# Two loads of the first expert layer: from SyncE's queue to GpSimd's

## The chip, the cores and the metric

The kernel runs on one core of one Trainium2 chip. The metric is the device time of one execution in microseconds. Before the change it is 3697.25 us, the median of three runs (3697.02 to 3698.64).

## What is computed

The reference runs two blocks of two layers each over 256 tokens of 1024 values. The part that matters here is the expert stage (`peer_ffn`) of the first block. Each token picks, for each of 8 heads, 16 of 16384 experts; expert e has a row `u[e]` and a row `v[e]`, and the stage adds `sum over the picked e of gate(t, e) * gelu(x(t) . u[e]) * v[e]`. In the first layer it runs for 512 tokens (256 of the sequence, 256 of the context), in the second for 256.

```
q = (xc @ w_q).reshape(PEER_CHUNK, PEER_HEADS, 2, PEER_HALF)
...
top_s, pos = lax.top_k(cand, PEER_TOPK)
eidx = jnp.take_along_axis(cidx, pos, axis=-1)
gate = jax.nn.softmax(top_s, axis=-1)
u = u_emb[eidx]
hid = jax.nn.gelu(jnp.einsum('td,thkd->thk', xc, u))
wgt = (gate * hid.astype(jnp.float32)).astype(xc.dtype)
return jnp.einsum('thk,thkd->td', wgt, v_emb[eidx])
```

## The kernel before, in words

**Dense and gathered tokens.** In the first layer 384 of the 512 tokens take the dense way: the hidden values of all 16384 experts are computed and multiplied with a matrix of gates that is zero where an expert wasn't picked. The other 128 tokens (NROW) take the gathered way, class `Rows`: their 16 x 8 picked rows of u, and later of v, are fetched one vector of 128 rows at a time by an indirect DMA on GpSimd's (POOL's) queue (`fetch`, line 258, 512 KB each). There are 128 fetches of u-rows, each followed by a dot product on DVE (L274), and then 128 fetches of v-rows, each pair followed by eight small matmuls on TensorE into `ps_row` (L307). There are five row buffers (ROWBUFS). Each fetch is made to wait for the matmul that was issued last at its place in the program (`pace_by`, `beat`), so that it goes out with TensorE's progress. In the second layer there are no gathered tokens, and `self.rows` is None there.

**Jobs.** The dense way goes through 64 jobs of 256 experts. A job needs the hidden values `hs` (128 x 768 for 384 tokens), the gates G for the same experts, and 1 MB of v weights. For 42 jobs (NLEAD) hs is computed early, while the picks are made, and stored to DRAM (`lead`, `hd`). The gates are built as one-hot products and stored to DRAM in blocks of 32 tokens (`gd`). The values loop then runs over the jobs: `prep` loads hs (L1209) or computes it from 1 MB of u weights (`hidden`, 22 jobs), multiplies it with G and splits the product into Wh and Wl on ScalarE and DVE; `values` multiplies these with the v weights (L1269). Jobs come in pairs, in turn a computed and a loaded one until the computed ones are used up, then loaded ones alone. One load of G (`gates`, L1556) serves a pair of jobs. In the first layer it moves 768 KB in runs of 512 bytes; there are 32 such loads, the first of which (704 KB, before `self.gcur` is set) is issued on POOL's queue in both layers and the rest on SP's.

**Buffers.** hs, G, Wh and Wl have two buffers each. Weights go through raw buffers (`wload`, L351): two, and in this loop a third. A raw buffer is free again when ScalarE has made the high part and DVE the low part of both its halves (L361, L362). The weights of the next stage's modulation pass through the same buffers (L624).

**What sets the order.** The program is written as one sequence; a planner at build time puts each engine's instructions in an order by its own estimate of when their operands are ready, and adds waits on semaphores. Each engine, and each queue of DMA issues, then works in that order. SP issues nothing but DMAs, and before the change its queue holds the u, v and modulation weights and the loads of hs and G. All SP transfers are in DMA queue q1 of the trace, POOL's in q0, and ScalarE's in q10.

Of the kernel before, what the change touches and what calls it, by code (L numbers as in the profile page):

```python
# [329 lines left out]
class Prog:  # L330
# [869 lines left out]
    def prep(self, l, b, xh, xl, T, gd, hd):  # L1200

        nc = self.nc
        G = self.gates(l, b, gd, T // GSTAGE, T)
        hs = self.hsp.tile([P, 2, T], F32, tag="hs", name="hs_r", bufs=2)
        if b >= NLEAD[l]:
            for _ in self.hidden(l, b, xh, xl, T, hs):
                pass
        else:
            nc.sync.dma_start(hs, hd[b])  # L1209
        Wh = self.pp.tile([P, 2, T], F32R, tag="Wh", name="Wh", bufs=2)  # L1210
        Wl = self.pp.tile([P, 2, T], F32R, tag="Wl", name="Wl", bufs=2)
        w = hs.rearrange("p j (q t) -> p j q t", t=GSTAGE)
        nc.vector.tensor_tensor(w, w, G.rearrange("p q j t -> p j q t"), op=ALU.mult)  # L1213
        self.split(Wh, Wl, hs)
        return Wh, Wl
# [334 lines left out]
    def gates(self, l, b, gd, nq, T):  # L1550
        nc = self.nc
        key = (l, b // 2)
        if self.gcur is None or self.gcur[0] != key:
            G = self.pp.tile([P, nq, 4, GSTAGE], F32, tag="G", name="G", bufs=2)
            n = nq if self.gcur else nq - 1
            (nc.sync if self.gcur else nc.gpsimd).dma_start(G[:, :n].rearrange("p q j t -> p q (j t)"),  # L1556
                              gd[:n, :, (b // 2) * 4:(b // 2) * 4 + 4, :].rearrange("q p j t -> p q (j t)"))
            if n < nq:
                nc.gpsimd.tensor_copy(G[:, n], self.glast)
            self.gcur = (key, G)  # L1560
        return self.gcur[1][:, :, (b % 2) * 2:(b % 2) * 2 + 2, :]
# [367 lines left out]
```

## Time and profile before

| what | value |
|---|---|
| median of the runs | 3697.25 us |
| the profiled execution | 3701.45 us, of which the span of instructions is 3699.7 us |
| TensorE (PE) busy | 3574.0 us, 97% of the span, 21681 matmuls |
| DVE, ScalarE (ACT), POOL busy | 2461.5, 1634.3, 604.0 us |
| DMA | 777.60 MB, mean 210 GB/s |
| q1 (SP), q0 (POOL), q10 (ScalarE), share of 16 engines | 43.7%, 10.4%, 5.0% |
| chain that ended last | PE 41%, DVE 4%, DMA 2%, the rest below that |
| mean granted TensorE clock | 0.985 of full speed |

The values loop of the first layer lies between 1190 and 2100 us of the span. In a row of the timeline, the first number is the start in us and the second the duration, and the bracket is the idle time of the engine before it and what ended it. In a row of the table of groups, the numbers behind the bar are busy time in us, mean ns of one, and idle time before. A granted clock of 1.00 is 2.4 GHz.

### The profile page before, as it was taken

The numbers are of one execution on the slowest core, as the hardware profiler recorded it, in microseconds if no ns is written. First come the engines' busy times: TensorE is split into PE (matmuls) and PEld (weight loads), VectorE is DVE, ScalarE is ACT, GpSimd is POOL, SyncE is SP. The second block draws the span as 40 slices with busy tenths as digits, with TensorE's granted clock in tenths as the row PEclk, the third lists the DMA queues.
The fourth block names the chain that finished last, engine by engine and source line by source line (L and its number), as shares of the span: only waits on it lengthen the run. The fifth ranks groups of instructions, "written<-read, shape, count | busy, mean of one in ns | idle before, by whom it ended". The sixth has DMA issues, their size and how long they took to land.

```text
span 3699.7 us, 55016 instructions
## 1 busy us (share of the span) xinstructions
PE 3574.0 (97%) x21681; PEld 3097.0 (84%) x21681; DVE 2461.5 (67%) x4540; ACT 1634.3 (44%) x2608; POOL 604.0 (16%) x686
## 2 busy tenths in 40 slices
PE   7999999899999998999999999999999999999999
PEld 5988877789999877776766799999998888887787
DVE  5566556599697777744445677778876555557675
ACT  3334333336576322222222354555676444445454
POOL 0112222100011232322222121221000000002121
PEclk9999999999999999999999999999999999999999
DMA  5222145224689898888889533354578766766453
GB/s 212 75 86 80 69 154 216 75 83 170 228 323 336 315 332 306 325 295 309 298 321 325 188 115 120 120 175 160 200 269 292 244 236 237 242 231 212 145 174 111
DMA packets 227763, 777.60 MB, mean 210 GB/s; under 512 B 17296, under 2 KB 100752, under 8 KB 168496
## 3 DMA queue, kind: packets, MB, share of 16 engines
q1 hardware_dynamic: 165984, 567.29, 43.7%
q0 software_dynamic: 37184, 135.41, 10.4%
q10 hardware_dynamic: 24336, 71.38, 5.0%
q8 instruction: 170, 2.79, 0.3%
q14 instruction: 89, 0.73, 0.1%
HBM read 705.60 MB, written 68.42 MB: 209 GB/s over the span
## 4 chain that ended last, share of the span: by engine, by line
PE 41%; DVE 4%; DMA 2%; ACT 1%; issue 1%; POOL 1%; DVEq 0%; ACTq 0%; SPq 0%; POOLq 0%
PE keep L1269 12%; PE ps_mm L393 5%; PE ps_mm L395 5%; PE ps_mm L394 5%; PE ps_wide L395 2%; PE ps_wide L393 2%; PE ps_wide L394 2%; PE ps_v L1269 1%; DVE ulo L362 1%; PE ps_nar L393 1%; PE ps_nar L395 1%; PE ps_nar L394 1%; DMA wraw<-in_v 1%; PE ps_mm L414 1%; PE ps_row L307 1%
## 5 line engine op out<-in xcount | busy, mean ns | idle before, releaser
L361 ACT ACTIVATE uhi<-wraw 128x1024 fp32r<-128x1024 f32 x586 | 609.0, 1057 | 879.2 <-PE ps_mm L394 336.1
L393 PE MATMUL ps_mm<-xh,uhi 128*128 128x256 f32 (+2 forms) x2952 | 955.5, 324 | 9.2 <-ACT hs L1566 3.7
L395 PE MATMUL ps_mm<-xh,ulo 128*128 128x256 f32 (+2 forms) x2952 | 940.8, 319 | 7.1 <-DVE ulo L362 7.1
L362 DVE TENSOR_TENSOR ulo<-wraw,uhi 128x1024 fp32r<-128x1024 f32 x586 | 718.0, 1237 | 340.6 <-ACT uhi L361 317.6
L394 PE MATMUL ps_mm<-xl,uhi 128*128 128x256 f32 (+2 forms) x2952 | 939.9, 318 | 0.0
L393 PEld LDWEIGHTS ps_mm<-xh,uhi 128*128 128x128 f32 x2952 | 562.5, 191 | 54.0 <-issue 9.2
L395 PEld LDWEIGHTS ps_mm<-xh,ulo 128*128 128x128 f32 x2952 | 562.2, 191 | 29.4 <-DVE ulo L362 8.0
L394 PEld LDWEIGHTS ps_mm<-xl,uhi 128*128 128x128 f32 x2952 | 562.7, 191 | 20.8
L362 DVE TENSOR_TENSOR vlo<-wraw,vhi 128x1024 fp32r<-128x1024 f32 x184 | 224.0, 1222 | 187.7 <-ACT vhi L361 187.5
L361 ACT ACTIVATE vhi<-wraw 128x1024 fp32r<-128x1024 f32 x184 | 193.2, 1056 | 338.1 <-DMA wraw<-in_v 176.0
L1269 PE MATMUL keep<-vlo,Wh 128*128 128x512 f32 x656 | 256.7, 391 | 3.6 <-DVE vlo L362 3.6
L1269 PE MATMUL keep<-vhi,Wh 128*128 128x512 f32 x656 | 257.8, 393 | 0.5 <-ACT Wh L422 0.5
L1269 PE MATMUL keep<-vhi,Wl 128*128 128x512 f32 x656 | 256.2, 391 | 0.3 <-DVE Wl L423 0.3
L258 POOL DMA_INDIRECT row<-in_urow,eu x128 | 158.5, 1238 | 589.7 <-PE ps_mm L395 440.7
L1213 DVE TENSOR_TENSOR hs_r<-hs_r,G 128x768 f32<-128x768 f32 (+1 forms) x128 | 105.2, 823 | 170.7 <-DMA hs_r<-hd 106.9
L393 PE MATMUL ps_nar<-uhi,xh 128*128 128x256 f32 x704 | 201.3, 286 | 2.3 <-ACT cs L664 2.3
L394 PE MATMUL ps_nar<-ulo,xh 128*128 128x256 f32 x704 | 200.1, 284 | 0.0
L395 PE MATMUL ps_nar<-uhi,xl 128*128 128x256 f32 x704 | 199.9, 284 | 0.0
L258 POOL DMA_INDIRECT row<-in_vrow,ev x128 | 136.0, 1063 | 375.4 <-PE keep L1269 180.2
L1530 ACT ACTIVATE stage<-ps_g 128x512 f32<-128x512 f32 x160 | 165.1, 1160 | 1.7 <-DMA wraw<-in_u 0.8
L274 DVE CUSTOM_DVE_ANT_0 row<-row,xt 128x1024 f32<-128x1024 f32 x128 | 155.2, 1219 | 4.5 <-DMA row<-in_urow,eu 4.5
L1269 PEld LDWEIGHTS keep<-vhi,Wh 128*128 128x128 f32 x656 | 123.7, 189 | 36.8 <-issue 9.2
(428 smaller groups left out, 6965.2 us busy)
## 6 DMA issues: line engine op xcount, KB each, us to landing
wraw<-in_u SPq DMA_DIRECT2D x128, 1024.0 KB
wraw<-in_v SPq DMA_DIRECT2D x128, 1024.0 KB
wraw<-in_wa SPq DMA_DIRECT2D x104, 1024.0 KB
wraw<-in_wb SPq DMA_DIRECT2D x50, 1024.0 KB
gd<-stage ACTq DMA_DIRECT2D x80, 512.0 KB
wraw_m<-in_wmod SPq DMA_DIRECT2D x24, 1024.0 KB
G<-gd SPq DMA_DIRECT2D x31, 768.0 KB
mraw<-in_wmod SPq DMA_DIRECT2D x16, 1024.0 KB
```

The source lines that it names most:

```text
L258: ins = self.nc.gpsimd.indirect_dma_start(row, None, self.p.g[name], bass.IndirectOffsetOnAxis(ap=idx, axis=0))
L274: ins = nc.vector.tensor_tensor_reduce(out=row, in0=row, in1=self.xt, op0=ALU.mult, op1=ALU.add, scale=1.0, scalar=0.0, accum_out=self.hid ...
L307: nc.tensor.matmul(ps[c:c + 32, :], m[:, g, :], rows[n - 4 + g][:, h * 512:(h + 1) * 512], start=(i == 0), stop=(i == 31), tile_position=( ...
L361: nc.scalar.activation(hi, r, AF.Copy)
L362: nc.vector.tensor_tensor(lo, r, hi.bitcast(F32), op=ALU.subtract)
L393: nc.tensor.matmul(ps, lh, rh, start=(i == 0), stop=False)
L394: nc.tensor.matmul(ps, lh, rl, start=False, stop=False)
L395: self.beat = nc.tensor.matmul(ps, ll, rh, start=False, stop=(i == n - 1))
L414: self.nc.tensor.matmul(ps[:, t0:t1], a[:, s], b[:, k, t0:t1], start=(n == 0 and i == 0), stop=(n == KD - 1 and i == 2))
L1213: nc.vector.tensor_tensor(w, w, G.rearrange("p q j t -> p j q t"), op=ALU.mult)
L1269: self.beat = self.nc.tensor.matmul(ps, a[:, j, t], b[:, c], start=(start and j == 0 and i == 0), stop=(stop and j == 1 and i == 2), skip_ ...
L1530: nc.scalar.activation(st[:, :, tb:tb + 4].rearrange("p j t -> p t j"), pg, AF.Copy, scale=1.0 / GSCALE)
```

## The change

Two issues go from SP's queue to POOL's where there are gathered tokens, that is in the first layer alone: the load of the early hidden values hs (42 loads of 384 KB) and the load of the gates G (the 31 loads of 768 KB that were SP's). The weights stay on SP. The second layer is as before.

```
@@ prep
         else:
-            nc.sync.dma_start(hs, hd[b])
+            (nc.gpsimd if self.rows else nc.sync).dma_start(hs, hd[b])
@@ gates
-            (nc.sync if self.gcur else nc.gpsimd).dma_start(G[:, :n].rearrange("p q j t -> p q (j t)"),
+            (nc.sync if self.gcur and not self.rows else nc.gpsimd).dma_start(G[:, :n].rearrange("p q j t -> p q (j t)"),
                               gd[:n, :, (b // 2) * 4:(b // 2) * 4 + 4, :].rearrange("q p j t -> p q (j t)"))
```

## Rows read from the trace of the kernel before

**Rows 1.** Table of stretches: us, engines' busy us, clock, DMA share, GB/s
```profile
1190.00:1600.00 410.00, 380.35 (x1817) 322.60 (x1816) 290.33 (x393) 122.28 (x150) 127.09 (x104) 0.96 0.87 317
1600.00:2100.00 500.00, 490.81 (x2417) 343.14 (x2416) 239.12 (x328) 131.71 (x153) 131.77 (x126) 0.99 0.86 305
```

**Rows 2.** Timeline of PE, first and last stall of the first half
```profile
1273.98 0.69 PE L393 MATMUL ps_mm<-xh,vhi 128*128 128x384 f32 x1 [4.47 <-DVE racc L1236]
...
1578.67 0.42 PE L393 MATMUL ps_mm<-xh,vhi 128*128 128x384 f32 x1 [3.13 <-ACT uhi L361]
```

**Rows 3.** Timelines of DVE and ACT at the first stall, and a later load
```profile
1256.30 0.96 DVE L1213 TENSOR_TENSOR hs_r<-hs_r,G 128x768 f32<-128x768 f32 x1 [2.59 <-DMA hs_r<-hd]
...
1269.88 2.00 ACT L361 ACTIVATE uhi<-wraw 128x1024 fp32r<-128x1024 f32 x2 [9.23 <-DMA wraw<-in_v]
...
1585.82 1.06 ACT L361 ACTIVATE vhi<-wraw 128x1024 fp32r<-128x1024 f32 x1 [2.16 <-DMA wraw<-in_v]
```

**Rows 4.** Timeline of SP's issues before the first and the last stall
```profile
1248.46 0.33 SPq L1209 DMA_DIRECT2D hs_r<-hd  x1
...
1257.29 0.37 SPq L1556 DMA_DIRECT2D G<-gd  x1
1261.85 0.35 SPq L351 DMA_DIRECT2D wraw<-in_v  x1
...
1561.53 0.37 SPq L1556 DMA_DIRECT2D G<-gd  x1
1564.94 0.33 SPq L351 DMA_DIRECT2D wraw<-in_u  x1
...
1580.83 0.33 SPq L351 DMA_DIRECT2D wraw<-in_v  x1
```

**Rows 5.** Waits of SP's queue, 1190 to 2110: us in total, times, longest
```profile
SPq L1556 <- DVE hs_r L1213: 120.0, 20, 8.9
SPq L1209 <- DVE Wl L423: 112.7, 26, 10.1
```

**Rows 6.** DMA queues, 1257 to 1262 us: packets, MB, share of 16 engines
```profile
DMA packets 1831, 1.74 MB, mean 348 GB/s; under 512 B 47, under 2 KB 1602, under 8 KB 1830
...
q1 hardware_dynamic: 1570, 0.80, 58.1%
q0 software_dynamic: 260, 0.93, 48.6%
```

**Rows 7.** DMA queues, 1190 to 1200 us, with POOL's one G
```profile
DMA packets 1048, 3.98 MB, mean 398 GB/s; under 512 B 113, under 2 KB 113, under 8 KB 979
...
q0 software_dynamic: 480, 1.77, 47.5%
```

**Rows 8.** Timelines: two gathers on POOL, and who waited for them
```profile
1288.85 1.71 POOL L258 DMA_INDIRECT row<-in_urow,eu  x1 [0.30 <-issue]
...
1298.05 1.23 DVE L274 CUSTOM_DVE_ANT_0 row<-row,xt 128x1024 f32<-128x1024 f32 x1 [2.37 <-DMA row<-in_urow,eu]
...
1671.37 1.38 POOL L258 DMA_INDIRECT row<-in_vrow,ev  x1 [1.36 <-PE keep L1269]
...
1682.20 1.06 PE L307 MATMUL ps_row<-row,mask 128*32 128x512 f32 x6 [0.65 <-DMA row<-in_vrow,ev]
```

**Rows 9.** Groups by line, POOL
```profile
L258 POOL DMA_INDIRECT row<-in_vrow,ev x128 | 136.0, 1063 | 375.4 <-PE keep L1269 180.2 <-PE ps_v L1269 87.3 <-PE ps_mm L395 81.2
```

**Rows 10.** POOL's G of the second layer: its issue, and q0 from 2832.7 to 2838
```profile
2828.54 1.07 POOL L1556 DMA_DIRECT2D G<-gd  x1 [235.11 <-PE ps_g L1528]
...
q0 software_dynamic: 128, 0.46, 28.8%
```

**Rows 11.** Timelines of POOL and PE near the end of the loop
```profile
1999.73 1.40 POOL L258 DMA_INDIRECT row<-in_vrow,ev  x1 [2.94 <-PE keep L1269]
...
2008.85 1.06 PE L307 MATMUL ps_row<-row,mask 128*32 128x512 f32 x8
```

**Rows 12.** DMA issues from 1586 to 2110 us: count, KB each
```profile
G<-gd SPq DMA_DIRECT2D x18, 768.0 KB
```

## The prediction

> **What bounds the kernel now.** I read the table of stretches over the values loop of the first layer first, because the two edited lines act only there (1190 to 2100 us). The reader is to see two halves [rows 1]. From 1190 to 1600 us, where the rest of the hidden values is computed and the u-rows are fetched, TensorE is idle for 410 - 380.35 = 29.7 us, and its granted clock averages 0.96: part of the time it stands at 1.2 GHz instead of 2.4, which loses another 0.04 x 410 = 16.4 us. From 1600 to 2100 us it is idle for 9.2 us and the clock is 0.99. So what faster loads can give lies in the first half: 29.7 us, and at most 16.4 us of clock on top.
>
> Next, TensorE's timeline, for who ended the idle times. There are six stall places in the first half, one in every four jobs; the first lasts 4.47 us, the last ends with 3.13 us [rows 2]. Some name a DVE add on racc, some the split of a weight. DVE and ScalarE at the first place show that both are one thing: ScalarE waits 9.23 us for a v weight [rows 3], DVE, which works in order, waits for ScalarE, and so can't free the accumulator. SyncE's timeline shows the late weight [rows 4]: the v load was issued at 1261.85, 4.2 us after a load of G (1257.29 + 0.37), and was used at 1269.88, 8.0 us after its issue. A v load with no G just ahead took from 1580.83 to 1585.82, 5.0 us [rows 3, 4]. All six places have a G issued 1 to 5 us ahead of the late weights, as in the first (1257.29, 1261.85) and the last (1561.53, 1564.94) [rows 4].
>
> **What the change does, part by part.** Sums are made against the profiled execution, 3701.45 us, which lies 4.2 us over the median of 3697.25 us; the difference is taken off at the end.
>
> *Removed from SP:* 42 issues of hs and 31 of G. SP's wait for the buffer of G was 120.0 us in 20 cases and for that of hs 112.7 us in 26 cases [rows 5]. One would expect the weights behind them to gain that. They don't: after the wait for G that ended at 1257.29 the weight still waited until 1261.85 for its own raw buffer. I take 0 for the issue waits; the bounds are 0 and the 29.7 us of idle time, as more can't be given back.
>
> *Weights no longer behind G in the transfer queue (q1).* While G moves, q1 has 1570 packets in 5 us, nearly all of the 512-byte kind (under 2 KB less under 512 B is 1555), and they fill 58.1% of 16 engines: 0.581 x 5 us x 16 / 1570 = 30 ns each [rows 6]. A whole G is 768 KB, 1536 of them, 2.9 us of all engines, which it shares with the gathered rows in q0. A weight issued behind G waits for it. Without G it should take between 5.0 and 8.0 us; as the rows, and G itself in q0, still compete, I take 2.0 of the 3.0 us. Six places: -12 us (bounds 0 and -18). If the stalls get shorter, some stretches at 1.2 GHz go too: I take -3 us (bounds 0 and -16.4).
>
> *G in q0.* The one G of this layer that POOL issues already moves without any packet between 512 B and 2 KB: q0 has 480 packets in 10 us at 47.5%, 158 ns each, 3.7 KB on average [rows 7]. 768 KB in packets of 4096 B are 192, or 192 x 158 / 16 = 1.9 us. So G costs 1 us less of the DMA engines, 31 us over 910 us; I count it as part of the 2.0 us above. G's own landing has time: its buffer becomes free when the pair of jobs before last is through, so a pair of jobs lies between, 2 x 910 / 64 = 28 us.
>
> *hs in q0.* Here the load is needed at once: DVE's product of hs and G waited 2.59 us for a load that was issued at 1248.46 and used at 1256.30, 7.8 us later [rows 3, 4]. In q0 the nearest price is that of a gathered row that was waited for: 1288.85 to 1298.05, 9.2 us [rows 8]. POOL may also be in a gather when hs becomes free, 1.06 us each [rows 9]. Against it stands that hs no longer queues behind a 1 MB weight in q1. Bounds per place: -2.6 us (the wait goes wholly) and +1.4 + 1.1 = +2.5 us. I take +1.0 us, since POOL's in-order queue is sure and the faster landing is not: six places, +6 us (bounds -16 and +15).
>
> *Added to POOL:* 73 issues of about 1.1 us [rows 10], 80 us of an engine that has 375.4 us of idle time before the v gathers alone, mostly waiting for TensorE's beat [rows 9]. The issues cost nothing by themselves; without that cover they would cost up to 80 us. What costs is order. POOL is in order, so behind an hs or G that waits for its buffer stand the row gathers, and behind these DVE's dot products (u half) and TensorE's ps_row matmuls (v half), both in order too. And in q0 a gather stands behind the data of G. From the G that POOL issues in the second layer: issue at 2828.54, and its 128 packets (448 KB are 112, and 16 that signal) lie between 2832.7 and 2838 us, so the first moved about 4.2 us after the issue [rows 10]. A gather issued 1 to 3 us after a G, the spacing of the gathers, would then find q0 taken for 2 to 4 us more than now.
>
> The slack of a gather: near the end, one issued at 1999.73 is used at 2008.86, 9.1 us later [rows 11]. Landing took 9.2 and 10.8 us in two cases in which somebody waited [rows 8], and must take less in the others, as almost nobody waits for a row now. So the slack is a few us for the later row of a pair and more for the other. 18 loads of G fall in the second half [rows 12], where TensorE itself waits; I assume that at one in four the gather is late by 1.5 us: +7 us (bounds 0, and 18 x 4 = 72 us if every G delayed a row without slack). In the first half DVE absorbs it.
>
> Sum: -12 - 3 + 6 + 7 = -2 us, so 3699.5 us for the profiled execution and 3695 us for the median.
>
> **A rule against the change.** The trace shows q1 and q0 moving at once, 58.1% and 48.6% of the 16 engines in the same 5 us: nothing is idle for a second queue to use [rows 6]. The Trainium skill, "DMA: Bandwidth & Descriptors", section "Issuing engines are not separate DMA queues", says that the DMAs of all issuing engines end on the same 16 DMA engines and that several issuers save only the time to issue. By this rule the -12 and -3 would be 0; with no cost for the rows the time would stay at 3697 us, the third rival below. Where rule and rows part is the packet size, which here differs with the issuer (30 ns packets against 158 ns).
> The Trainium skill's same page, section "Latency and other measured facts", gives a first byte after about 1 us for POOL's path and 0.6 us for SP's. An estimate by it would make the hs term 6 x 0.4 = 2.4 us and the sum -5.6 us. The 4.2 us of [rows 10] are far above that, and the measurement decides.
>
> **Rivals.**
> 1. *The weights win.* The six stalls shrink by 2.5 us each (-15), with them go stretches at 1.2 GHz worth 1 us per place (-6), hs is hardly later than now (+2) and late rows cost 4 us: -15, 3682 us. For it: the late loads of all six places stand behind a G. Against: the DMA engines are at 0.87 in that half [rows 1], so something else must be later.
> 2. *The rows pay (slower).* One mechanism: a G at the head of POOL's queue and of q0 holds back the gathers behind it. It decides from the point where the delay exceeds the few us of slack. With a lateness of 1.5 us at each of the 18 places before TensorE, and not at every fourth, it costs 27 us, and with the +6 of hs, less the 15 of the weights, the sum is +18: 3715 us. For it: SP's waits for these buffers were up to 8.9 and 10.1 us long [rows 5], and POOL would take them over unless the planner puts the gathers ahead. Against: POOL is mostly waiting for TensorE anyway.
> 3. *Hidden anyway.* The same engines move the same bytes, and the stalls stay: 3697 us.
>
> **How the numbers follow.** Near balance as summed: 0.38, 3695 us, own range 3688 to 3704. Weights win: 0.28. Rows pay: 0.24. Hidden anyway: 0.10. The range that should hold 8 in 10 reaches into both sides, 3680 to 3713 us. A measurement of this kernel can tell about 0.2%, 7.4 us, from no change. Faster by more: the 0.28 and 0.04 of the first case. Slower by more: 0.24. Between: the other 0.34 of the first case and the 0.10, so 0.44.
>
> **What will show it.** In the profile after, the packets of 512 B to 2 KB must be gone from q1 between 1190 and 2100 us; if not, the change doesn't do what it says. TensorE's idle time in the first half tells the weights' step: 17 to 20 us if I am right, near 10 if the weights win. TensorE's waits at ps_row tell the rows' step: hardly anything now, about 7 us expected, over 20 if the rows pay. DVE's wait for hs should grow from 2.59 to about 3.6 us in the place shown. What would make the forecast wrong most easily is POOL's order as the planner sets it: it decides whether a waiting G stands in front of a gather, and the profile of before can't show it.

## The result: slower, 3750 us

| | before | after |
|---|---|---|
| median | 3697.94 us (3697.02 to 3702.35, 4 runs) | 3750.40 us (3746.25 to 3753.52, 4 runs) |
| ratio | | 1.0139, interval 1.0121 to 1.0156 |
| profiled execution, span | 3701.45, 3699.7 us | 3749.08, 3747.3 us |
| mean granted clock | 0.985 | 0.982 |

The forecast was 3695 us with a range up to 3713. The time lies beyond both; of the rivals the second, "the rows pay", had the sign and the place, but with +18 us where +52 came.

The page of the kernel after, the packets of the whole execution and DVE's product of hs and G: busy time, mean ns, idle time before and what ended most of it.
```profile
DMA packets 183411, 777.60 MB, mean 208 GB/s; under 512 B 17296, under 2 KB 53136, under 8 KB 124144
...
L1213 DVE TENSOR_TENSOR hs_r<-hs_r,G 128x768 f32<-128x768 f32 (+1 forms) x128 | 104.9, 823 | 234.5 <-DMA hs_r<-hd 173.2
```
The change did what it says. The packets from 512 B to 2 KB went from 100752 - 17296 in the page of before to 53136 - 17296: 47616 are gone, 31 loads of G by 1536. No byte more or less was moved. DVE's product, for which a load from DRAM is needed at once, had waited 106.9 us for hs; now it waits 173.2.

The table of stretches of after, in the columns of [rows 1]:
```profile
1190.00:1600.00 410.00, 368.93 (x1747) 314.02 (x1747) 282.85 (x382) 117.01 (x143) 147.85 (x124) 0.95 0.85 307
1600.00:2100.00 500.00, 470.28 (x2262) 322.82 (x2260) 218.09 (x301) 122.22 (x142) 163.46 (x164) 0.97 0.82 290
```
Against [rows 1] TensorE's idle time rose from 29.7 to 41.1 us in the first half and from 9.2 to 29.7 us in the second: 32 us. The granted clock fell from 0.96 to 0.95 and from 0.99 to 0.97: 0.01 x 410 + 0.02 x 500 = 14 us. Together some 46 of the 47.6 us between the two profiled executions (the clock has two digits, so the 14 us are rough). The loop as a whole says the same: from its first product of hs and G to its last, DVE's timelines have 1236.45 to 2081.96 before and 1237.06 to 2130.89 in after, 48.3 us more. So the loss lies in this loop. On the average of the loop DMA moves fewer bytes per second than before; in single places its engines are full, as shown below.

The waits of after from 1190 to 2150 us (engine, line, what it waited for: us in total, times, longest):
```profile
DVE hs_r L1213 <- DMA hs_r<-hd: 145.2, 31, 10.5
ACT Wh L422 <- DVE hs_r L1213: 89.9, 26, 11.8
...
POOL G L1556 <- DVE hs_r L1213: 86.1, 21, 8.4
...
POOL hs_r L1209 <- DVE Wl L423: 53.0, 12, 12.3
...
PE ps_row L307 <- DMA row<-in_vrow,ev: 26.3, 8, 9.3
```
SP's waits for the two buffers [rows 5] are POOL's now, 86.1 and 53.0 us. TensorE waits 26.3 us at `ps_row` for gathered rows; 25.0 us of it fall between 1600 and 2100, most of the 29.7 us that it is idle there. Before, the same view had 0.9 us there and 84.3 us for DVE's first line.

The first stall place of the first half in after, timelines of DVE, POOL, SP, ACT and PE, which answer to [rows 2 to 4]:
```profile
1259.64 0.96 DVE L1213 TENSOR_TENSOR hs_r<-hs_r,G 128x768 f32<-128x768 f32 x1 [1.95 <-DMA hs_r<-hd]
...
1260.90 1.07 POOL L1556 DMA_DIRECT2D G<-gd  x1 [3.88 <-DVE hs_r L1213]
...
1265.19 0.33 SPq L351 DMA_DIRECT2D wraw<-in_v  x1
...
1273.35 2.00 ACT L361 ACTIVATE uhi<-wraw 128x1024 fp32r<-128x1024 f32 x2 [11.74 <-DMA wraw<-in_v]
...
1277.46 0.69 PE L393 MATMUL ps_mm<-xh,vhi 128*128 128x384 f32 x1 [7.33 <-DVE racc L1236]
```
G is out of q1, and the v weight still needs 1273.35 - 1265.19 = 8.2 us to its use, 8.0 before. TensorE's stall grew from 4.47 to 7.33 us, though DVE's wait for hs just before it fell from 2.59 to 1.95.

The heart of it is a place in the second half: POOL's timeline in after, then DVE's and PE's.
```profile
1904.98 0.61 POOL L1209 DMA_DIRECT2D hs_r<-hd  x1
...
1917.34 0.58 POOL L1209 DMA_DIRECT2D hs_r<-hd  x1 [9.23 <-DVE Wl L423]
...
1923.24 1.07 POOL L1556 DMA_DIRECT2D G<-gd  x1 [4.06 <-DVE ulo L362]
1924.62 0.97 POOL L258 DMA_INDIRECT row<-in_vrow,ev  x1 [0.30 <-issue]
1925.89 1.45 POOL L258 DMA_INDIRECT row<-in_vrow,ev  x1 [0.30 <-issue]
1927.69 0.59 POOL L1209 DMA_DIRECT2D hs_r<-hd  x1 [0.35 <-DVE Wl L423]
...
1943.13 0.58 POOL L1209 DMA_DIRECT2D hs_r<-hd  x1 [12.35 <-DVE Wl L423]
...
1914.02 0.96 DVE L1213 TENSOR_TENSOR hs_r<-hs_r,G 128x768 f32<-128x768 f32 x1 [8.47 <-issue]
...
1939.18 0.96 DVE L1213 TENSOR_TENSOR hs_r<-hs_r,G 128x768 f32<-128x768 f32 x1 [10.52 <-DMA hs_r<-hd]
...
1948.26 0.96 DVE L1213 TENSOR_TENSOR hs_r<-hs_r,G 128x768 f32<-128x768 f32 x1 [5.42 <-DMA hs_r<-hd]
...
1937.03 1.93 PE L307 MATMUL ps_row<-row,mask 128*32 128x512 f32 x6 [9.34 <-DMA row<-in_vrow,ev]
```
The table of stretches over this place, in the columns of [rows 1]:
```profile
1925.00:1939.00 14.00, 4.66 (x17) 1.54 (x15) 3.66 (x5) 0.00 (x0) 4.52 (x5) 0.68 1.00 362
1939.00:1943.00 4.00, 4.00 (x18) 2.40 (x19) 3.34 (x5) 0.85 (x1) 0.00 (x0) 0.85 0.20 80
```
Read it as a ring. An hs load that went out at 1904.98, 3.1 us behind a G, is used at 1914.02, 9.0 us later, when it has just landed, and DVE has stood 8.47 us. Only when its product is split is a buffer of hs free: POOL waits 9.23 us with the next hs load at its head (1917.34). The product of that one starts at 1920.83, and G, released by a DVE instruction just behind it, goes out at 1923.24, with the gathers behind it. Within 5 us POOL issues G, two gathers and hs, 768 + 2 x 512 + 384 KB in one queue, and two more gathers right after. For 14 us all 16 DMA engines are full (share 1.00), of which weights in q1 take 38.8%. The hs load is used 11.5 us after its issue (1927.69 to 1939.18); by the packets in the trace 7.9 of these pass before its first one moves, against 1.3 us for the load of 1917.34, with no G just ahead. DVE stood 10.52 us for it, and TensorE 9.34 us for a gather of the same batch, one of the two ahead of hs. Until that product is split, POOL waits 12.35 us with the next hs load at its head, and the DMA engines fall to a share of 0.20. Then the next batch goes out. The next hs load has no G ahead of it: 1943.13 to 1948.26, 5.1 us.

### The profile page after: what moved, and what is told of

It is laid out like the page before. It is cut to its first block, busy times and chain, and to the rows that moved or that the text cites. A ratio compares the mean times of both kernels' runs of the same rounds, so it can differ in the third digit from the quotient of the medians.

```text
span 3747.3 us, 55026 instructions
## 1 busy us (share of the span) xinstructions
PE 3583.9 (96%) x21681; PEld 3097.1 (83%) x21681; DVE 2459.6 (66%) x4540; ACT 1633.9 (44%) x2608; POOL 669.7 (18%) x759
## 2 busy tenths in 40 slices
DMA packets 183411, 777.60 MB, mean 208 GB/s; under 512 B 17296, under 2 KB 53136, under 8 KB 124144
## 3 DMA queue, kind: packets, MB, share of 16 engines
q0 software_dynamic: 46992, 176.31, 13.8%
## 4 chain that ended last, share of the span: by engine, by line
PE 75%; DMA 9%; DVE 7%; issue 5%; ACT 3%; POOL 2%; ACTq 0%; POOLq 0%; SPq 0%; DVEq 0%
PE keep L1269 14%; PE ps_mm L393 12%; PE ps_mm L394 12%; PE ps_mm L395 12%; DMA wraw<-in_v 3%; PE ps_v L1269 3%; PE ps_nar L393 2%; PE ps_nar L395 2%; PE ps_nar L394 2%; PE ps_wide L395 2%; PE ps_wide L394 2%; PE ps_wide L393 2%; PE ps_mm L414 2%; DMA hs_r<-hd 2%; DVE ulo L362 2%
## 5 line engine op out<-in xcount | busy, mean ns | idle before, releaser
L1213 DVE TENSOR_TENSOR hs_r<-hs_r,G 128x768 f32<-128x768 f32 (+1 forms) x128 | 104.9, 823 | 234.5 <-DMA hs_r<-hd 173.2
L422 ACT ACTIVATE Wh<-hs_r 128x768 fp32r<-128x768 f32 (+1 forms) x128 | 93.2, 728 | 156.9 <-DVE hs_r L1213 98.5
```

The lines of the kernel that those rows point to most:

```text
L422: nc.scalar.activation(hi, src, AF.Copy)
```

## The experiments

Three theories stood at the start. A: it is the waiting. POOL waits for a buffer at the head of its queue, and the gathers behind it go out late. B: it is the data. G and hs lie in q0 ahead of the gathers, which land late. C: hs itself lands late from POOL, and DVE, in order, waits for it; then hs alone would cost nearly everything and G alone nothing. All runs are three rounds against the kernel before; "hs" and "row" are DVE's wait for hs and TensorE's wait for a gathered row from 1190 to 2150 us (before: 84.3 and 0.9).

| run | median us | ratio, interval | hs, us | row, us |
|---|---|---|---|---|
| G alone on POOL | 3717.79 | 1.0045 (1.0028 to 1.0063) | 111.0 | 7.0 |
| hs alone on POOL | 3710.05 | 1.0029 (1.0018 to 1.0040) | 89.8 | 1.3 |
| the waits alone on POOL | 3697.31 | 0.9993 (0.9981 to 1.0005) | 78.4 | 2.1 |
| both on ScalarE's queue | 3723.89 | 1.0061 (1.0037 to 1.0084) | 142.5 | 0.3 |
| both cut, on POOL | 3672.16 | 0.9935 (0.9919 to 0.9952) | 118.8 | 2.0 |
| both cut, on SP | 3667.30 | 0.9916 (0.9899 to 0.9933) | 81.4 | none |
| both on POOL, paced | 3758.57 | 1.0155 (1.0131 to 1.0178) | 173.4 | 1.9 |
| hs cut, G whole, on POOL | 3736.19 | 1.0100 (1.0078 to 1.0122) | 145.2 | 22.4 |
| the same cut on SP | 3687.35 | 0.9969 (0.9954 to 0.9984) | 97.2 | 0.3 |
| G cut, hs whole, on POOL | 3685.48 | 0.9965 (0.9952 to 0.9979) | 109.2 | 5.3 |
| the same cut on SP | 3663.75 | 0.9910 (0.9891 to 0.9929) | 66.8 | 0.2 |
| after, gathers earlier | 3746.47 | 1.0127 (1.0108 to 1.0146) | 162.4 | 13.1 |
| before, gathers earlier | 3690.36 | 0.9973 (0.9962 to 0.9984) | 81.7 | none |
| after, hs ahead of G | 3708.25 | 1.0026 (1.0012 to 1.0040) | 110.4 | 5.7 |
| before, hs ahead of G | 3693.09 | 0.9985 (0.9975 to 0.9995) | 79.4 | 0.5 |
| before, both orders | 3683.17 | 0.9967 (0.9954 to 0.9980) | 75.0 | none |

**Each half of the change alone.** One of the two lines of the diff at a time.

> Only the loads of G go to POOL's queue; hs stays on SP. Theory A (order: a load that waits for its buffer at the head of POOL's in-order queue holds back the row gathers): in the kernel after, POOL stood 86 us before G and 65 us before hs, so G should carry somewhat more than half of the 52 us: 3720 to 3730 us, with PE waits on ps_row of 10 to 18 us. Theory B (queue: the gathers' rows stand behind the data of G and hs in q0): G is 24 of the 40 MB moved, so 3725 to 3735 us. Theory C (hs lands late from POOL, and DVE, in order, waits for it): no loss, 3690 to 3700 us.

> Only the loads of hs go to POOL's queue; G stays on SP. Theory A: the smaller half, 3712 to 3725 us. Theory B: 16 of 40 MB, 3710 to 3720 us. Theory C: nearly the whole loss, 3735 to 3750 us, with DVE's wait for hs at 145 us as in the kernel after against 84 us before.

Against the 3700.9 us of before measured beside them, G alone costs 17 us and hs alone 9. Theory C in this form fell with both; A and B came within 7 us of both times, so these two runs don't part them. Both lines do harm, but 26 is half of 52: the two do something to each other.

**The waits without the data.** The loads stay on SP; POOL writes one column of the buffer ahead of each load, and so has to wait for the buffer as in the changed kernel, with gathers behind it.
```diff
-            nc.sync.dma_start(hs, hd[b])
+            (nc.gpsimd.memset(hs[:, 0, 0:1], 0.0) if self.rows else None, nc.sync.dma_start(hs, hd[b]))
...
-            n = nq if self.gcur else nq - 1
+            n = (nc.gpsimd.memset(G[:, 0, 0, 0:1], 0.0) if self.rows else None, nq)[1] if self.gcur else nq - 1
```


> Both loads stay on SP; POOL writes one column of the buffer ahead of each (0.1 us), so POOL's queue has the same 73 waits and q0 has not one byte more. Theory A: near the kernel after, 3730 to 3755 us, with PE waits on ps_row of over 15 us. Theory B: as the kernel before, 3695 to 3705 us, ps_row waits under 3 us.

Waits of that kernel, 1190 to 2150 us (its edit sits one line higher for G, L1555):
```profile
POOL G L1555 <- DVE hs_r L1213: 56.7, 18, 10.2
POOL hs_r L1209 <- DVE Wl L423: 48.9, 17, 8.9
```
POOL waits 106 us in these two lines, up to 10.2 us at a time, and it costs nothing: 3697.31 us. That is less waiting than the 139 us of after, where the waits also feed on the delay, and the planner's order on TensorE is not quite that of before (50 of 21681 matmuls stand elsewhere); but theory A in its plain form fell here.

**Another queue.** Both loads from ScalarE's queue (`nc.gpsimd` replaced by `nc.scalar` in the two lines).

> Both loads go to ScalarE's queue, whose transfers are q10: off SP's queue, but not on POOL's. Theories A and B: no gather is held back, ps_row waits near 1 us as before; but ScalarE is in order and takes the 73 waits ahead of the weights' splits, so the time may still rise, 3700 to 3740 us. If instead taking the loads out of q1 were itself what costs, it would be 3750 us with ps_row waits as in the kernel after. If weights gain from leaving G (my forecast's step), v loads behind G should land in 5 to 6 us instead of 7.5.

No gather is late (0.3 us), yet 23 us are lost, with DVE's wait for hs as long as in after. So there is a loss without any late gather. That the late hs makes it is not shown: ScalarE, in order, also has its own splits of weights behind the loads that wait.

**Little data.** Of each hs load the last 32 of 384 columns and of each G the first of 12 blocks are moved and read again for the rest, once with both loads on POOL and once on SP.
```diff
-            (nc.gpsimd if self.rows else nc.sync).dma_start(hs, hd[b])
+            (nc.gpsimd if self.rows else nc.sync).dma_start(hs[:, :, T - GSTAGE if self.rows else 0:], hd[b][:, :, T - GSTAGE if self.rows else 0:])
...
-            n = nq if self.gcur else nq - 1
+            n = (1 if self.rows else nq) if self.gcur else nq - 1
```


> As the kernel after, but each load is cut to a twelfth: G loads its first block of 32 tokens alone (64 KB), hs its last 32 columns (32 KB), and the product reads these over and over, so the output isn't the reference's. POOL's queue keeps its 73 issues and their waits, q0 loses 37 of the 40 MB. The first two runs and the wait-alone run so far speak for theory B in this form: a gather that stands behind a G in q0 lands about 3 us later (8.4 to 9.4 us median against 5.4 to 6.0), and only together with the late issue is the slack gone. Then this kernel has ps_row waits under 3 us and is as fast as the same cut on SP's queue (e6), within 8 us. By theory A in its strict form it would be 40 us or more slower than that.

> The same cut, with the order of the kernel before (loads on SP): the pair of e5, and a bound on what these 40 MB cost in the kernel before. My forecast's step (weights wait behind G, six stalls of 2 us and some clock) says 3680 to 3687 us. If the six stalls have another cause (the DMA engines are full with whatever is there, or DVE's order), 3690 to 3700 us. If all the idle time of the first half goes, 3655 us.

With the data gone POOL's queue costs 3672.16 - 3667.30 = 5 us instead of 52, although POOL's waits are still there:
```profile
POOL G L1556 <- DVE hs_r L1213: 55.5, 23, 6.1
...
POOL hs_r L1208 <- DVE Wl L423: 37.0, 18, 6.2
```
The pair says one thing more: the traffic of G and hs costs some 31 us on SP's queue too (3698 to 3667). That is more than my forecast's step allowed for (3680 to 3687 us).

**No waiting POOL.** Both loads, on POOL, are made to wait for TensorE's beat as the gathers do, so that their buffers are free when they reach the head.
```diff
+            ins = (nc.gpsimd if self.rows else nc.sync).dma_start(hs, hd[b]); self.rows and self.rows.pace_by(ins, mybir.DependencyClass.Sync)
...
+            self.rows and self.gcur and self.rows.pace_by(ins, mybir.DependencyClass.Sync)
```


> As the kernel after, with all data, but each load on POOL waits for TensorE's beat as the gathers do, so it stands in program order among them and its buffer should be free when its turn comes: POOL's waits for buffers (151 us after) nearly gone. Theory B alone (data in q0): ps_row waits stay above 15 us and the time above 3735 us. If it takes both the late issue and the data, ps_row waits fall under 8 us; but hs is then issued later than it could be, and DVE's wait for it grows, so the time is 3705 to 3735 us.

A miss that taught something. The gathers are on time (1.9 us in the table), and in the waits hs is later than ever:
```profile
ACT Wh L422 <- DVE hs_r L1212: 335.1, 57, 16.4
DVE hs_r L1212 <- DMA hs_r<-hd: 173.4, 34, 10.8
PE keep L1268 <- ACT Wh L422: 68.1, 20, 9.3
```
TensorE lost its 68.1 us at the split of the late product. Here hs is late because its issue waits for the beat, so this is not the loss of after; but after this run the late gathers alone no longer explained a loss of that size.

**Which data.** One load cut, the other whole, on POOL and on SP.

> The changed kernel with hs cut alone: each hs load brings its last 32 columns (32 KB of 384), read again for the other columns; G is loaded whole, both on POOL. If the data of G in q0 holds the gathers back: ps_row waits stay over 7 us and the time lies at 3700 to 3720 us (the +17 of G alone, less some 13 us that the missing traffic gives). If G and hs together are needed, one load standing behind the other: 3675 to 3700 us and ps_row under 4 us. DVE's wait for hs should fall from 145 to about 90 us.

> Control of the run in which hs is cut and G is whole on POOL (3736 us): the same cut, both loads on SP. If what was seen there is the price of the queue and not of the cut: 3680 to 3700 us, so a price of 36 to 56 us; if the cut's own order is bad: over 3715 us.

> The changed kernel with G cut alone: each load of G brings its first block of 32 tokens (64 KB of 768), read again for the other tokens; hs is loaded whole, both on POOL. If the data of G is what holds the gathers and hs back: ps_row under 3 us, DVE's wait for hs at 90 to 110 us and 3675 to 3695 us. If hs behind a waiting G is the larger part, by POOL's order and not by data: hs wait stays over 130 us and the time at 3705 to 3735 us.

> Control of the run in which G is cut and hs is whole on POOL (3685 us): the same cut, both loads on SP. If the price of POOL's queue is small once G is small: 3672 to 3685 us, so 0 to 13 us; if hs on POOL has a price of its own whatever G does, as the 9 us of hs alone and more: under 3665 us.

POOL's queue costs 3736.19 - 3687.35 = 49 us with G whole and hs cut, and 3685.48 - 3663.75 = 22 us with hs whole and G cut (the members on POOL stand beside runs of before at 3701.57 us, those on SP beside 3699.60 us). My numbers for hs cut on POOL were far off, since I took the bytes of hs for a part of the cause. The price is 52 us with both whole, 49 with hs cut, 22 with G cut, 5 with both cut: it goes mostly with G's bytes. The bytes of hs count for 3 us beside a whole G and for 17 beside a cut one (22 against 5), so hs on POOL has a price of its own. And the full price needs hs issued from the same queue, since G alone costs 17. POOL's timeline and DVE's with hs cut to 32 KB:
```profile
1918.18 1.07 POOL L1556 DMA_DIRECT2D G<-gd  x1 [4.18 <-DVE mask L300]
...
1925.43 0.75 POOL L1208 DMA_DIRECT2D hs_r<-hd  x1
...
1939.31 0.75 POOL L1208 DMA_DIRECT2D hs_r<-hd  x1 [10.62 <-DVE Wl L423]
...
1934.55 0.96 DVE L1213 TENSOR_TENSOR hs_r<-hs_r,G 128x768 f32<-128x768 f32 x1 [9.80 <-DMA hs_r<-hd]
...
1944.27 0.96 DVE L1213 TENSOR_TENSOR hs_r<-hs_r,G 128x768 f32<-128x768 f32 x1 [5.26 <-DMA hs_r<-hd]
```
A load of 32 KB, 7 us behind a G and with three gathers between, is used 1934.55 - 1925.43 = 9.1 us after its issue; the next one, with no G ahead, after 5.0. It waits for what stands ahead of it and not for its own bytes. This gave a fourth theory, the ring: hs, issued behind a G and needed first, is late; POOL, held by the buffer that the late hs keeps, holds the next hs, the next G and the gathers; and so G and hs do harm together.

**Are the gathers the way of the loss?** Each gather waits for the matmul at the place of the gather before it, in after and in before.
```diff
-        self.pace_by(ins, mybir.DependencyClass.Sync)
+        self.pace_by(ins, mybir.DependencyClass.Sync, True)
...
+        beat, self.last = (getattr(self, 'last', self.p.beat), self.p.beat) if early else (self.p.beat, self.last); ...
```


> The changed kernel with each gather made to wait for the matmul at the place of the gather before it, so that it can go out some 3.5 us earlier. If the loss goes through gathers that land late: ps_row falls from 26 to under 12 us and the time from 3750 to 3715 to 3735 us. If the late hs and the DVE work behind it are the way of the loss: ps_row falls too, but the time stays at 3742 to 3756 us.

> The kernel before with the same earlier gathers: the control of the run ahead. Nobody waits for a gather there (ps_row 0.9 us), so 3692 to 3705 us by the first theory; a rival says that gathers put earlier collide with the weights and cost 5 to 15 us: 3702 to 3712 us.

After's wait at `ps_row` is halved, 13.1 us, and the time falls by 4 us; the wait went to hs:
```profile
DVE hs_r L1212 <- DMA hs_r<-hd: 162.4, 32, 12.4
```
Against its control (3690.36) the changed kernel still loses 56 us. So `ps_row` is where TensorE's loss shows, and not by itself what has to be mended. The control itself beats both kernels, 0.9973 of before.

**hs ahead of G.** Everything of the change stays on POOL; each G is only put behind the last hs load issued before it in the program, as an order without a semaphore.
```diff
+            self.hsin = (nc.gpsimd if self.rows else nc.sync).dma_start(hs, hd[b])
...
+            self.rows and hasattr(self, 'hsin') and self.tc.add_manual_dep(ins.ins, self.hsin.ins.name, mybir.DependencyInfo(mybir.DependencyClass.NoSync, ...), reason="pace")
```


> The changed kernel with each G put behind the hs load before it in POOL's order, so that hs no longer stands behind 768 KB of G and two gathers. If q0 moves its data in the order of issue and hs pays for standing last (8.2 us in the median behind a G, 5.0 us without): DVE's wait for hs falls from 145 to 100 to 120 us and the time to 3710 to 3735 us. If the gathers behind G are the loss, G now being no earlier for them: ps_row stays over 15 us and the time over 3740 us.

3708.25 us: 42 of the 52 us are back, with the same loads from the same queue. POOL's and DVE's timelines, at a place like the one above:
```profile
1911.96 0.58 POOL L1208 DMA_DIRECT2D hs_r<-hd  x1 [7.86 <-issue]
1912.52 1.09 POOL L1555 DMA_DIRECT2D G<-gd  x1
1913.91 1.01 POOL L258 DMA_INDIRECT row<-in_vrow,ev  x1 [0.30 <-issue]
...
1922.85 0.59 POOL L1208 DMA_DIRECT2D hs_r<-hd  x1 [2.61 <-DVE Wl L423]
...
1915.98 0.96 DVE L1212 TENSOR_TENSOR hs_r<-hs_r,G 128x768 f32<-128x768 f32 x1 [5.55 <-DMA hs_r<-hd]
```
hs is used 4.0 us after its issue, not 11.5, and POOL's next hs load waits 2.61 us, not 12.35. The waits of this kernel:
```profile
DVE hs_r L1212 <- DMA hs_r<-hd: 110.4, 24, 9.6
POOL hs_r L1208 <- DVE Wl L423: 62.1, 24, 6.4
...
POOL G L1555 <- DVE hs_r L1212: 15.6, 9, 2.6
...
PE ps_row L307 <- DMA row<-in_vrow,ev: 5.7, 6, 2.9
```
The two places are not equal in all: here hardly any weights move in q1 while hs does. The sums over the loop carry the argument. The gathers still stand behind G, and they land no sooner for it: issued less than 4 us behind a G they take 9.2 us in the median (9.7 in after), the others 6.4 (6.8), worked out from the trace. Yet TensorE waits 5.7 us for them and not 26.3. What fell is POOL's wait for the buffer of G ahead of them, from 86.1 to 15.6 us. So I read that the gathers in after were late by both: they stood behind G's data, and they were issued late, behind a G that waited for an hs that was late itself.

Is that a cure for POOL's queue, or would the order help anywhere? The same edit in the kernel before, and the same with the earlier gathers:

> Control of the run with hs ahead of G on POOL (3708 us): the same order given to the kernel before, both loads on SP. Counted from the issue of hs to the product that waited for it, a G issued less than 7 us ahead makes 7.8 us of 4.0 in the kernel before as well (9.1 of 4.4 after), so a late hs is not POOL's alone. If the order is what the 42 us are and only POOL turns a late hs into held gathers: before gains little, 3685 to 3700 us, and DVE's wait for hs falls from 84 to 65 to 80 us. If the order gives the same 42 us wherever the loads stand, the queue's price is the same as ever: 3650 to 3665 us.

> The kernel before with both orders, hs ahead of G and each gather waiting for the matmul at the place of the gather before it (alone 3690 us). If the two add: 3675 to 3692 us. If hs ahead of G does nothing on SP, as the late hs there holds nobody back: 3686 to 3696 us.

On SP the order is worth 4 us (3693.09 against 3696.95). TensorE's order of instructions is the same in before, in after and in both kernels with hs ahead. DVE's is not: in after the planner put nine of the 64 products of hs and G one to four instructions later than in the kernel with hs ahead on POOL. DVE stood idle before all nine, eight times with the load of hs as what ended it, so it is not DVE's order that made them late; what the other order cost elsewhere was not separated. Yet the late hs is there in the kernel before as well; its SP, POOL and DVE timelines at the like place:
```profile
1917.28 0.38 SPq L1556 DMA_DIRECT2D G<-gd  x1
...
1920.47 0.32 SPq L1209 DMA_DIRECT2D hs_r<-hd  x1
...
1924.64 0.94 POOL L258 DMA_INDIRECT row<-in_vrow,ev  x1 [4.44 <-PE keep L1269]
1928.62 0.94 POOL L258 DMA_INDIRECT row<-in_vrow,ev  x1 [3.05 <-PE keep L1269]
...
1930.21 0.96 DVE L1213 TENSOR_TENSOR hs_r<-hs_r,G 128x768 f32<-128x768 f32 x1 [7.22 <-DMA hs_r<-hd]
```
An hs behind a G is used 9.7 us after its issue, DVE waits 7.22 us, and meanwhile POOL's gathers go out, each with TensorE's beat. In the kernel after, the same lateness holds the next G and hs at POOL's head, and gathers behind them. That is the main difference of the two kernels in one view. Another is that in after 18 of the 42 hs loads go out less than 7 us behind a G, and in before 13. With hs ahead of G, POOL's queue still costs 3708.25 - 3693.09 = 15 us; what these are was not separated (hs alone on POOL costs 9). Both orders together on SP give 3683.17 us, the fastest of the kernels that leave nothing out, though its interval overlaps that of the earlier gathers alone.

## Why the prediction was wrong, by its own steps

- **Weights no longer behind G in q1 (-12, and -3 of clock): failed.** I read the 8.0 us of the first v weight as 5.0 us and 3 us of G ahead of it. Without G in q1 it took 8.2 us, and TensorE's idle time of the first half rose. What I called a cause, a G just ahead in the same queue, was no matter of the queue. G's bytes count, on either queue: the first half with G cut, on SP and then on POOL:
```profile
1190.00:1600.00 410.00, 396.18 (x1941) 332.94 (x1940) 301.60 (x409) 126.67 (x155) 137.82 (x109) 0.98 0.85 313
...
1190.00:1600.00 410.00, 391.39 (x1896) 330.12 (x1895) 294.91 (x400) 127.53 (x156) 146.41 (x136) 0.98 0.84 308
```
  TensorE is idle for 13.8 and 18.6 us there, where it is 29.7 before and 41.1 in after; with G whole and alone on POOL it is 34.4. The clock, from which I took 3 us back, went from 0.96 to 0.95 instead. The rule that I had set against the change, that issuers share the DMA engines (the Trainium skill, "DMA: Bandwidth & Descriptors", "Issuing engines are not separate DMA queues"), gave 0 for this term, and the trace agrees.
- **hs in q0 (+6): the sign right, the size and the mechanism wrong.** This is the step on which the sum failed. I priced it from a gather that had no G ahead, at six places of the first half. It acts in both halves: DVE's wait for hs went from 84.3 to 145.2 us. In the place that I named it even fell, from 2.59 to 1.95 us. I had looked at how long hs takes and not at whom a late hs holds up. Nor were the 4.2 us from issue to first packet of [rows 10] a price of POOL's path: the hs load of 1917.34, with no G just ahead, moves its first packet 1.3 us after its issue.
- **Late rows (+7): mis-sized.** TensorE waits 26.3 us at `ps_row` and the clock falls by 0.02 beside it. "A G holds back the gathers" was half of it (a G's data costs them some 3 us of landing, with little harm by itself: 7.0 us at `ps_row` with G alone on POOL); I had put hs and the gathers in two separate terms, each with its own bounds, where they are members of one ring: late hs, late split, buffer not free, POOL held, late next hs, late G and late gathers.
- **"The issues cost nothing by themselves": right**, as the waits alone cost nothing (3697.31).
- **"G's own landing has time": right**; in the waits DVE's product stands for hs, and in no line for G.
- **Rival 2** had the sign and the place with a third of the size, and half of the mechanism: a G did wait at POOL's head, 86.1 us in all, but for the late hs, which the rival counted apart. The bound of my term for late rows, 18 x 4 = 72 us, would have held the result; the range should have reached towards it, as no row excluded it. I named POOL's order as the thing that I could not see, and gave it too little weight in the range.

## What to carry to other kernels

In an in-order queue put the load that is needed soonest ahead of the large one that has time; here that alone is worth 42 us where gathers stand in the same queue, and 4 us where none do. Moving loads off a busy queue need not make what stays any faster: here the same 16 engines moved the same bytes, and the weight shown took 8.2 us instead of 8.0. Where one load's buffer is freed by the work that waits for that load, two costs that look separate can come to more than their sum (52 us against 17 and 9): price them as a ring, with the longest wait that a row shows, and not as a sum of averages.

## What the runs showed that I had not expected

- What stands ahead of a load weighs more than its size. From the issue of hs to the product that waited for it it took 9.1 us in the median with a G issued less than 7 us ahead, and 4.0 us without one (18 and 14 cases in after before which DVE stood idle, worked out from the trace); with hs cut to 32 KB it was 8.2 and 3.9 us, and in the kernel before, on SP's queue, 7.8 and 4.0 us.
- The medians from issue to landing in after, 1190 to 2110 us, hide all of this:
```profile
wraw<-in_v SPq DMA_DIRECT2D x63, 1024.0 KB, 7.7
...
hs_r<-hd POOLq DMA_DIRECT2D x40, 384.0 KB, 6.5
row<-in_vrow,ev POOLq DMA_INDIRECT x122, 7.3
```
  With G alone on POOL they are 8.0, 8.1 and 7.2 us, and that kernel is 33 us faster: the median landing doesn't tell which load was in whose way.
- 106 us of waiting at the head of POOL's queue cost nothing, and 1/12 of the bytes made the same queue nearly free (5 us).
